# First layer's gate and up projections by seven quarter products, and the modulation as sets of four float32 products on TensorE

## Chip, cores and metric

The kernel runs on one core of a Trainium2 chip. The metric is device time in microseconds (us), the median of three runs; less is better.

## What is computed

One denoising step of a two-layer trunk on 512 latent and 128 context tokens (640 in all), width 1024, float32. Each layer first maps a conditioning vector to six modulation vectors of 1024 values, once for the latent tokens and once for the context tokens:

```python
sh1, sc1, g1, sh2, sc2, g2 = jnp.split(mod, N_MOD, axis=-1)
h = rmsnorm(x, prm['norm1_g'][l]) * (1 + sc1) + sh1
cols = jnp.einsum('bnd,de->bne', h, prm['w_in'][l])
...
mix = jnp.einsum('bne,ed->bnd', jnp.concatenate([ya, yb, yc], axis=-1), prm['w_out'][l])
x = x + g1 * mix
h = rmsnorm(x, prm['norm2_g'][l]) * (1 + sc2) + sh2
gate, up = jnp.split(jnp.einsum('bnd,df->bnf', h, prm['w_gu'][l]), 2, axis=-1)
x = x + g2 * jnp.einsum('bnf,fd->bnd', jax.nn.silu(gate) * up, prm['w_down'][l])
```

Here `mod` is SiLU(conditioning) times `w_mod` (1024 x 6144 in each layer) plus a bias. Between `cols` and `mix` lie the mixers: a chunked gated delta rule with a short convolution, a spatial-gating branch and a pooling branch. The FFN's hidden width is 2816, which is 22 blocks of 128.

## The kernel before

Activations are kept transposed: 128 channels on the partitions, the 640 tokens along the free axis, worked on in halves of 320. A float32 weight block is split into a rounded part (`wh`) and a rest (`wl`), and so is an activation (`xhi`, `xlo`); a product is three fp32r passes (`mm3`, line 338). Each pass of a block of 128 x 128 weights over one half is one instruction on TensorE. Where the text says a plain pass, it means that.

The stages follow one another: prologue (load, transpose, first two sixths of the modulation), mixer of layer 0, output projection of layer 0 (line 1303), FFN of layer 0 (from line 1314), then the same three for layer 1 and a final norm. Instructions are placed on the engines' queues before the run by a scheduler that goes by priorities (`PRI`, program order) and its own picture of time; at run time each engine takes its queue in order. TensorE's chains of projections are kept in order among themselves by `behind` (line 169), and everything else is put between them.

**The FFN.** In layer 0 all 22 blocks are done one by one: gate (8 weight blocks x 3 passes x 2 halves) and up (the same), 96 passes a block, then `w_down` in pieces of 8, 8 and 6 blocks. In layer 1 two blocks are done in this way (`unit_old`, line 1416), two on normalised rows (`unit_plain`, line 1442), and the other 18 by `Unit` (line 1465), which forms gate and up of a block from seven quarter products P1 to P7 of 12 passes each, on sums of rows (`t_sums`) and sums of weight blocks (`prep`): 84 passes. There the down projection goes in pieces of 4, 4, 4, 5 and 5 blocks (`PIECES`).

**The modulation.** The prologue computes the first two sixths of layer 0 by `first_mod_` (line 502): 8 float32 products [128 x 32] x [128 x 512] in four column groups of the array, then four transposes and a sum over the groups on VectorE. The other ten sixths are 20 groups of 512 columns, each in 8 steps (`pump`, line 256): a tile `wm` of `w_mod` (256 KB) is loaded by SyncE's queue, VectorE multiplies and adds it into `ma` for the latent tokens, ScalarE multiplies it for the context tokens and GpSimd adds that. After 8 steps `mod_sums` reduces `ma`: by 8 transposes on TensorE outside the FFN, by VectorE transposes and 4 small products in it. `PUMPS` and `POUT` say behind which projections a step goes. `pump_to` completes what a stage needs. The last group is finished about half way through the FFN of layer 0.

Of the kernel before, what the change touches and what calls it, by code (L numbers as in the profile page):

```python
# [9 lines left out]
F32 = mybir.dt.float32  # L10
# [29 lines left out]
W32, WM, WHL = 2, 3, 2  # L40
# [55 lines left out]
def tile_hybrid_step(ctx: ExitStack, tc: tile.TileContext,  # L96
# [115 lines left out]
    quarters = const.tile([P, 32], F32, name="quarters")  # L212
# [11 lines left out]
    steps = [(l, w * D + c0, k) for l, w in SIXTHS for c0 in (0, 512) for k in range(KT)]  # L224
    ps_ = {"i": 0, "j": 0, "ma": None, "wm": {}, "due": None, "at": "mix0"}

    def mod_sums(l, c0, ma):
        t0 = c0 // P
        if ps_["at"] != "ffn0":
            for s in range(2):  # L230
                pt = md()
                for cb in range(4):
                    nc.tensor.transpose(pt[:, cb * P:(cb + 1) * P], ma[:, s, cb * P:(cb + 1) * P], ident)
                m = mod[:, l, s, t0:t0 + 4]
                nc.vector.tensor_reduce(m, pt.rearrange("p (c n) -> p c n", c=4), op=ADD, axis=AX.X)
                tt(m, m, bmod[:, l, t0:t0 + 4], ADD)
            mod_scales(l, c0)
            return

        ms = sm.tile([P, 2, 16], F32, tag="ms", name="ms", bufs=1)  # L240
        for s in range(2):
            pt = md()
            nc.vector.transpose(pt, ma[:, s])
            nc.vector.tensor_reduce(ms[:, s], pt.rearrange("p (c n) -> p c n", n=32), op=ADD, axis=AX.X)
# [3 lines left out]
        tt(mod[:, l, :, t0:t0 + 4], pt[:, 0:8].rearrange("p (s t) -> p s t", s=2),  # L248
           bmod[:, l, t0:t0 + 4].unsqueeze(1).to_broadcast([P, 2, 4]), ADD)
        mod_scales(l, c0)  # L250
# [5 lines left out]
    def pump(n=1):  # L256
        with at("pump"):
            pump_(n)

    def pump_(n):  # L260
        for _ in range(n):
            if ps_["due"] is not None:
                mod_sums(*ps_["due"])
                ps_["due"] = None
            i = ps_["i"]
            if i >= len(steps):
                return
            while ps_["j"] < min(len(steps), i + WM):
                l, c0, k = steps[ps_["j"]]
                wm = wp.tile([P, 512], F32, tag="wm", name="wm", bufs=WM)  # L270
                nc.sync.dma_start(wm, w_mod[l, k * P:(k + 1) * P, c0:c0 + 512])
                ps_["wm"][ps_["j"]] = wm
                ps_["j"] += 1
            l, c0, k = steps[i]
            wm = ps_["wm"].pop(i)
            if k == 0:
                ps_["ma"] = sm.tile([P, 2, 512], F32, tag="ma", name="ma", bufs=1)
            ma = ps_["ma"]
            if k == 0:
# [6 lines left out]
            if k == KT - 1:  # L286
                ps_["due"] = (l, c0, ma)
            ps_["i"] += 1

    def pump_to(l, w):  # L290

        n = 2 * KT * (SIXTHS.index((l, w)) + 1)
        while ps_["i"] < n:
            pump()
        if ps_["i"] == n and ps_["due"] is not None:
            mod_sums(*ps_["due"])
            ps_["due"] = None
# [53 lines left out]
    def gemm_xs(wb, xs, evac, pumps=(1, 1), done=None):  # L351


        for half in range(2):
# [14 lines left out]
            pump(pumps[half])  # L369

    def gemm_act(wb, ks, xs, evac, n=1):
        wh, wl = wb
        for half in range(2):
            sl = slice(half * HALF, half * HALF + HALF)
            o = acc()[:, 0:HALF]
            for i, k in enumerate(ks):
                hi, lo = xs[i]
                mm3(o, wh[k], wl[k], hi[:, sl], lo[:, sl], i == 0, i == len(ks) - 1)
            evac(o, half)
            pump(n)  # L380
# [77 lines left out]

    wsp = tc.alloc_tile_pool(name="wsh", bufs=1, side="right")
    with tc.tile_pool(name="xin", bufs=1) as xp:  # L460
# [24 lines left out]
        def wm_tile():  # L485
            return wp.tile([P, 512], F32, tag="wm", name="wm", bufs=WM)

# [14 lines left out]
        def first_mod_(ws, c0, pool):  # L502
            pm = md()
            for k in range(KT):
                g = 32 * (k % 4)
                mm(pm[g:g + 32, :], sc[:, k, :], ws[k], k < 4, k >= KT - 4, tile_position=(0, g))
            msb = pool.tile([P, 512], F32, tag="msb", name="msb", bufs=1) if pool else wm_tile()
            copy("msb", msb, pm, "v")
            pt = md()
            for cb in range(4):  # L510
                nc.tensor.transpose(pt[:, cb * P:(cb + 1) * P], msb[:, cb * P:(cb + 1) * P], ident)
            m = mod[:, 0, :, c0 // P:c0 // P + 4]
            nc.vector.tensor_reduce(m, pt.rearrange("p (cb g m) -> p m cb g", cb=4, g=4)[:, 0:2], op=ADD, axis=AX.X)
            tt(m, m, bmod[:, 0, c0 // P:c0 // P + 4].unsqueeze(1).to_broadcast([P, 2, 4]), ADD)
# [43 lines left out]
        nc.vector.tensor_reduce(quarters, ident.rearrange("p (g m) -> p m g", g=4), op=ADD, axis=AX.X)  # L558
# [13 lines left out]
        for k in range(KT):  # L572
            xk = xks[k]
            if k % 2:
                sq = xp.tile([P, NT], F32, tag="sq", name="sq", bufs=1)
            else:
                sq = sm.tile([P, 2, 512], F32, tag="ma", name="sq", bufs=1).rearrange("p s n -> p (s n)")[:, 0:NT]
# [20 lines left out]
    for l in range(DEPTH):  # L598
        xs = nrm.xs
        with ExitStack() as es:  # L600
# [50 lines left out]
            def gemm_in(c0, n, evac, key):  # L651
                wb, done = early.pop(c0, None) or (wcol(c0, n), None)
                gemm_xs(wb, xs, evac, PUMPS.get(f"{key}{l}", (0, 1)), done)

# [484 lines left out]
            def pool():  # L1139
                mark(f"pool{l}")  # L1140
                pT = on[2:4]
                for i in range(2):
                    gemm_xs(wcol(C_PP + i * P, P), xs, ev_act(pT[i], AF.Identity), PUMPS.get(f"pool{l}", (0, 1)))
# [28 lines left out]
            def branches():  # L1172
# [3 lines left out]
                for i in range(2):  # L1176
                    gemm_xs(wcol(C_VB + i * P, P), xs, ev_act(vT[i], AF.Gelu_apprx_tanh), PUMPS.get(f"sgu{l}", (0, 1)))
# [23 lines left out]
                for i in range(2):  # L1201
                    gemm_xs(wcol(C_U + i * P, P), xs, ev_act(uT[i], AF.Gelu_apprx_tanh), PUMPS.get(f"sgu{l}", (0, 1)))
# [17 lines left out]
                for h in range(NH):  # L1220
                    gemm_xs(wcol(C_Z + h * P, P), xs, ev_act(zs[h], AF.Silu), PUMPS.get(f"z{l}", (0, 1)))
# [65 lines left out]
        if l + 1 < DEPTH:  # L1287
            with tc.tile_pool(name=f"fx{l}", bufs=1, reuse_waits="tile") as xpool, tc.tile_pool(name=f"ft{l}", bufs=1, reuse_waits="tile") as ftp, tc.tile_pool(name=f"ff{l}", bufs=1, reuse_waits="tile") as fp:
                x = [xpool.tile([P, NT], F32, name=f"x{k}") for k in range(KT)]
                for n in range(KT):  # L1290
                    nc.scalar.dma_start(x[n], xd[n])

                def ft(name):
                    return ftp.tile([P, NT], F32, tag="ft", name=name, bufs=4)

                ps_["at"] = f"out{l}"
                pump_to(l, 2)
                pump_to(l, 4)
                nrm = Norm(l, 1)
                for n in range(KT):  # L1300
                    cs = slice(n * P, (n + 1) * P)
                    wb = wblock([(w_out[l, 4 * P:8 * P, cs], 0, 4), (w_out[l, 0:4 * P, cs], 4, 4)], 8, P)
                    gemm_act(wb, range(8), yb + ya, resid(l, 16, n, x[n]), POUT)
                    nrm.add(n, x[n], ft("sq"), shift=False)
                pump_to(l, 3)
                for n in range(KT):
                    nrm.shift(n)
                rst = nrm.finish()
                xs2 = nrm.xs
                mark(f"ffn{l}")  # L1310
                ps_["at"] = f"ffn{l}"
                pieces = (8, 8, 6)
# [429 lines left out]
```

## Time and profile before

| | before |
|---|---|
| median of 3 runs | 1706.49 us (1705.74 to 1706.92) |
| profiled execution, its own time | 1703.07 us |
| span of its instructions | 1701.3 us |
| TensorE busy | 1633.1 us, 96% |
| VectorE busy | 1263.5 us, 74% |
| ScalarE busy | 827.8 us, 49% |
| GpSimd busy | 505.3 us, 30% |

The profiled execution lies 3.4 us under the median. PE is TensorE, DVE VectorE, ACT ScalarE, POOL GpSimd, SP SyncE (which only issues DMAs). A pass is shown with a duration of about 310 ns, but one starts every 147 ns: passes are pipelined, so costs on PE are read from start to start.

### The profile page before, as it was taken

How to read it: one execution, taken by the hardware profiler on the slowest of the kernel's cores; microseconds unless marked ns; L12 is line 12 of the kernel's file. 1: busy time of each engine (PE TensorE's matmuls, PEld its weight loads, DVE VectorE, ACT ScalarE, POOL GpSimd, SP SyncE). 2: the span in 40 equal slices, each digit the busy share in tenths (PEclk: the TensorE clock that was granted, in tenths of full speed). 3: DMA queues.
4: the chain of work that ended last, by engine and by line, in shares of the span. 5: the costliest groups of instructions: out<-in, count | busy, mean ns of one | idle time of the engine just before them, and what ended most of it. 6: DMA issues, size and time to landing. Idle time of an engine off the chain costs nothing.

```text
span 1701.3 us, 33005 instructions
## 1 busy us (share of the span) xinstructions
PE 1633.1 (96%) x12736; PEld 1567.5 (92%) x12736; DVE 1263.5 (74%) x2618; ACT 827.8 (49%) x1712; POOL 505.3 (30%) x533
## 2 busy tenths in 40 slices
PE   6999999998999999999999999999999999999997
PEld 4788989888899999999998989899999999999997
DVE  6688687789988778887556876776586768585774
ACT  4467765544444344434335756734363435353453
POOL 4342330356654645555146212111410000000000
PEclk8999999999999999999999999999999999999999
DMA  9431221444544544444234111113321323322331
GB/s 319 151 99 46 82 82 39 118 155 124 155 143 136 158 135 142 143 149 130 72 106 115 45 39 51 43 39 89 107 75 53 102 63 106 87 75 62 100 100 62
DMA packets 243636, 174.34 MB, mean 102 GB/s; under 512 B 10262, under 2 KB 212632, under 8 KB 243480
## 3 DMA queue, kind: packets, MB, share of 16 engines
q1 hardware_dynamic: 232144, 157.45, 30.7%
q10 hardware_dynamic: 10184, 12.29, 2.2%
q0 software_dynamic: 1152, 2.51, 0.5%
q8 instruction: 100, 1.64, 0.4%
q14 instruction: 56, 0.46, 0.1%
HBM read 163.29 MB, written 8.91 MB: 101 GB/s over the span
## 4 chain that ended last, share of the span: by engine, by line
PE 51%; DVE 3%; ACT 1%; issue 1%; DMA 1%; POOL 0%; DVEq 0%; ACTq 0%; POOLq 0%
PE acc L121 39%; PE dl L121 11%; PE md L121 0%; DMA w<-in_w_down_dram 0%; DVE wl L126 0%; DVE cv L129 0%; PE dl L1694 0%; DMA w<-in_w_gu_dram 0%; POOL guh L835 0%; PE md L765 0%; DVE yt L129 0%; DVE Z L126 0%; DVE st L129 0%; DVE dl L126 0%; ACT MT L950 0%
## 5 line engine op out<-in xcount | busy, mean ns | idle before, releaser
L121 PE MATMUL acc<-xhi,wh 128*128 128x322 f32 (+2 forms) x1472 | 468.5, 319 | 5.4 <-DVE ga L126 4.5
L121 PE MATMUL acc<-xlo,wh 128*128 128x322 f32 (+2 forms) x1472 | 466.6, 317 | 1.3 <-DVE xlo L129 1.2
L121 PE MATMUL acc<-xhi,wl 128*128 128x320 f32 (+1 forms) x1440 | 456.7, 317 | 4.9 <-DVE wl L126 4.9
L329 POOL TENSOR_TENSOR wl<-w,wh 128x384 fp32r<-128x384 f32 x128 | 172.3, 1346 | 832.1 <-ACT wh L325 429.7
L325 ACT CAST wh<-w 128x1024 fp32r<-128x1024 f32 (+3 forms) x186 | 179.4, 964 | 258.9 <-PE acc L121 184.3
L121 PEld LDWEIGHTS acc<-xhi,wh 128*128 128x128 f32 (+1 forms) x1472 | 278.6, 189 | 10.7 <-PE acc L121 7.2
L121 PEld LDWEIGHTS acc<-xlo,wh 128*128 128x128 f32 (+1 forms) x1472 | 278.7, 189 | 3.8 <-POOL wl L329 1.5
L121 PEld LDWEIGHTS acc<-xhi,wl 128*128 128x128 f32 x1440 | 275.1, 191 | 6.5 <-DVE wl L126 5.9
L285 POOL TENSOR_TENSOR ma<-ma,wm 128x512 f32<-128x512 f32 x140 | 206.6, 1476 | 134.3 <-ACT wm L154 115.0
L126 DVE TENSOR_TENSOR wl<-w,wh 128x640 fp32r<-128x640 f32 (+3 forms) x186 | 201.3, 1082 | 46.0 <-issue 19.8
L121 PE MATMUL acc<-ah,wh 128*128 128x320 f32 (+2 forms) x644 | 198.9, 310 | 0.5
L121 PE MATMUL acc<-al,wh 128*128 128x320 f32 (+2 forms) x644 | 198.4, 308 | 0.0
L121 PE MATMUL acc<-ah,wl 128*128 128x320 f32 (+2 forms) x644 | 198.3, 308 | 0.0
L154 ACT ACTIVATE wm<-wm,sc 128x512 f32<-128x512 f32 x140 | 101.0, 722 | 136.0 <-DVE ma L129 113.8
L129 DVE SCALAR_TENSOR_TENSOR x<-acc,mod,x 128x128 f32<-128x128 f32 (+3 forms) x240 | 97.3, 434 | 85.0 <-PE acc L121 84.7
L129 DVE SCALAR_TENSOR_TENSOR ma<-wm,sc,ma 128x512 f32<-128x512 f32 x140 | 138.4, 988 | 23.9 <-DMA wm<-in_w_mod_dram 23.1
L121 PEld LDWEIGHTS acc<-ah,wh 128*128 128x128 f32 x644 | 120.7, 188 | 1.7 <-DVE ga L126 1.2
L121 PEld LDWEIGHTS acc<-al,wh 128*128 128x128 f32 x644 | 120.8, 188 | 0.1
L121 PEld LDWEIGHTS acc<-ah,wl 128*128 128x128 f32 x644 | 120.8, 188 | 0.0
L1482 ACT CAST sh<-sv 128x512 fp32r<-128x512 f32 x72 | 44.5, 620 | 36.1 <-PE dl L121 15.4
L1328 ACT CAST ah<-ga 128x320 fp32r<-128x320 f32 x44 | 20.2, 460 | 82.3 <-DVE ga L129 82.3
L129 DVE SCALAR_TENSOR_TENSOR ga<-up,bt,ga 128x320 f32<-128x320 f32 (+2 forms) x66 | 59.3, 924 | 1.3
(432 smaller groups left out, 3537.6 us busy)
## 6 DMA issues: line engine op xcount, KB each, us to landing
wm<-in_w_mod_dram SPq DMA_DIRECT2D x162, 256.0 KB, 2.9
w<-in_w_gu_dram SPq DMA_DIRECT2D x70, 512.0 KB, 3.8
w<-in_w_in_dram SPq DMA_DIRECT2D x44, 512.0 KB, 3.6
wu<-in_w_gu_dram SPq DMA_DIRECT2D x18, 512.0 KB, 3.8
w<-in_w_out_dram SPq DMA_DIRECT2D x32, 256.0 KB, 3.0
w<-in_w_down_dram SPq DMA_DIRECT2D x16, 512.0 KB, 4.3
wf<-in_w_mod_dram SPq DMA_DIRECT2D x30, 256.0 KB, 5.7
w<-in_w_down_dram SPq DMA_DIRECT2D x24, 256.0 KB, 2.6
```

Source lines behind the costliest of these rows:

```text
L121: return nc.tensor.matmul(o, lhsT=l, rhs=r, start=st, stop=sp, **kw).ins
L126: recent["v"] = nc.vector.tensor_tensor(o, a, b, op=op).ins
L129: recent["v"] = nc.vector.scalar_tensor_tensor(o, a, s, b, op0=op0, op1=op1).ins
L154: recent["a"] = nc.scalar.activation(o, i, f, **kw).ins
L285: nc.gpsimd.tensor_tensor(ma[:, 1], ma[:, 1], wm, op=ADD)
L325: nc.scalar.copy(wh, v)
L329: nc.gpsimd.tensor_tensor(wl[:, c:], v[:, c:], wh[:, c:], op=SUB)
L1328: nc.scalar.copy(hi[:, sl], ga[:, sl])
L1482: nc.scalar.copy(hi, w)
```

## The change

Layer 0's FFN is now done by the code of layer 1: two blocks by `unit_old`, two by `unit_plain`, 18 by `Unit`, with the same pieces. The last piece of layer 0 ends in a down projection that also feeds the next norm, as before.

The 20 modulation groups are no longer multiplied on VectorE, ScalarE and GpSimd. A group is 8 float32 products on TensorE in two sets of four, one product in each of four column groups of 32 (the form of `first_mod_`). The copy of the result to SBUF (`msb`, VectorE) is followed by four small products with a 0/1 matrix of 2 columns, which add the four column groups and transpose in one, and one addition on VectorE. The prologue uses the same tail. There are four `wm` buffers now, so the second set of a group can be loaded only when the first set has read its tiles. Within a set the tile that was loaded last is taken first. Groups go behind the mixers' projections (0.18 of a group behind each half: 8 groups in the mixer of layer 0, 7 in that of layer 1) and behind P6 of every fourth block in layer 0's FFN (5 groups).

```diff
-POUT = 1
-
-PUMPS = {'log0': (0, 0), 'k00': (0, 0), 'q00': (1, 2), 'sgu0': (1, 1), 'z0': (0, 1), 'v10': (1, 1), 'q10': (0, 0), 'v00': (1, 0), 'k10': (0, 1), 'pool0': (1, 0)}
+
+SHARE = (0.18, 0.18)
...
-W32, WM, WHL = 2, 3, 2
+W32, WM, WHL = 2, 4, 2
...
+    def mod_columns(ws, l, c0, msb):
+
+        pm = md()
+        prev = None
+        for i in range(KT):
+            k, g = i, 32 * (i % 4)
+            if ws is None:
+                if i % 4 == 0:
+                    mod_loads(4)
+                    four = [ps_["wm"].pop(0) for _ in range(4)]
+                k = i + 3 - 2 * (i % 4)
+                w = four[k % 4]
+            else:
+                w = ws[k]
+            m = mm(pm[g:g + 32, :], sc[:, k, :], w, i < 4, i >= 4, tile_position=(0, g))
+            if ws is None and i % 4:
+                behind(m, prev)
+            prev = m
+        copy("msb", msb, pm, "v")
+
         pt = md()
-        for a in range(4):
-            mm(pt[32 * a:32 * a + 32, 0:8], quarters, ms.rearrange("p s (t a) -> p a s t", a=4)[:, a], True, True, tile_position=(0, 32 * a))
...
+        for cb in range(4):
+            mm(pt[:, 2 * cb:2 * cb + 2], msb[:, cb * P:(cb + 1) * P], C("I16")[:, 0:2], True, True)
+        tt(mod[:, l, :, c0 // P:c0 // P + 4], pt[:, 0:8].rearrange("p (t s) -> p s t", s=2),
+           bmod[:, l, c0 // P:c0 // P + 4].unsqueeze(1).to_broadcast([P, 2, 4]), ADD)
...
+    def mod_loads(n):
+
+        while len(ps_["wm"]) < n and ps_["j"] < KT * len(groups):
+            l, c0 = groups[ps_["j"] // KT]
+            k = ps_["j"] % KT
+            wm = wm_tile()
+            nc.sync.dma_start(wm, w_mod[l, k * P:(k + 1) * P, c0:c0 + 512])
+            ps_["wm"].append(wm)
+            ps_["j"] += 1
...
-            if k == 0:
-                behind_recent("v", ts, ma[:, 0], wm, sc[:, k, 0:1], None, MUL)
-                behind_recent("a", times, f"pump{ps_['at']}", ma[:, 1], wm, sc[:, k, 1:2], "a")
-            else:
-                behind_recent("v", stt, ma[:, 0], wm, sc[:, k, 0:1], ma[:, 0], MUL, ADD)
-                behind_recent("a", times, f"pump{ps_['at']}", wm, wm, sc[:, k, 1:2], "a")
-                nc.gpsimd.tensor_tensor(ma[:, 1], ma[:, 1], wm, op=ADD)
...
+    def pump(share):
+
+        ps_["sum"] += share
+        while ps_["sum"] >= 1.0 - 1e-6:
+            ps_["sum"] -= 1.0
+            if ps_["i"] < len(groups):
+                pump_group()
...
-        if l + 1 < DEPTH:
...
-                pieces = (8, 8, 6)
...
+                    if l + 1 < DEPTH and j % 4 == 0:
+                        pump_group()
...
+                if final:
+                    pump_to(l + 1, 1)
+                    pump_to(l + 1, 0)
+                    nrm = Norm(l + 1, 0)
...
+                    if final:
+                        nrm.add(n, x[n], xpool.tile([P, NT], F32, tag="sqn", name="sqn", bufs=2))
+                        nc.scalar.dma_start(xd[n], x[n])
```

In the rows of the queues below, `acc`, `dl` and `md` are PSUM tiles; `xhi`, `xlo`, `rh`, `rl`, `tah`, `tal` activations or row sums; `wh`, `wl`, `sh` weights or weight sums.

TensorE's queue in the FFN of layer 0, before: projections, and the small products at the end of a modulation group.

```order
L121 MATMUL acc<-xlo,wh 128x322
L121 MATMUL acc<-xhi,wl 128x322
L121 MATMUL md<-ms,quarters 32x8 x4
L121 MATMUL acc<-xhi,wh 128x320
L121 MATMUL acc<-xlo,wh 128x320
```

The same stage now, at the second set of a group of `wm`. Its first set of four stands 35 rows above it, behind a P6, with 34 passes between.

```order
L120 MATMUL acc<-tah,sl 128x320
L120 MATMUL acc<-tah,sh 128x320
L120 MATMUL md<-wm,sc 32x512 x4
L120 MATMUL acc<-tal,sh 128x320
L120 MATMUL acc<-tah,sl 128x320
L120 MATMUL dl<-rh_5063,sh 128x320
L120 MATMUL dl<-rl_5064,sh 128x320
L120 MATMUL dl<-rh_5063,sl 128x320
L120 MATMUL dl<-rh_5065,sh 128x320
L120 MATMUL md<-cst,msb 128x2 x4
```

The small products have made way for the float32 sets and for four products of 2 columns. A set does not always stay together. TensorE's queue in the mixer of layer 0, now, inside the delta rule's chain (`R`, `QK`):

```order
L120 MATMUL acc<-xhi,wl 128x320
L120 MATMUL md<-wm,sc 32x512
L120 MATMUL dl<-R,QK 128x128
L120 MATMUL md<-wm,sc 32x512
L120 MATMUL dl<-R,QK 128x128
L120 MATMUL md<-wm,sc 32x512
L120 MATMUL dl<-R,QK 128x128
L120 MATMUL md<-wm,sc 32x512
L120 MATMUL dl<-R,QK 128x128
```

Here the four products of a set stand singly, each with a full-width product behind it. Of the 40 sets, 26 stand whole, 13 as one product and three, and this one as four single ones: 56 stretches in all.

SyncE's queue in the FFN of layer 0, now:

```order
L1386 DMA wu<-in_w_gu_dram 128x8x128
L296 DMA w_6218<-in_w_gu_dram 128x8x128
L261 DMA wm<-in_w_mod_dram 128x512 x8
L1386 DMA wu<-in_w_gu_dram 128x8x128
L296 DMA w_6359<-in_w_gu_dram 128x8x128
```

The first four of the eight loads wait for the first set on TensorE, the next four for the second set; the weight loads of the next blocks are queued behind them. Before, three or four such loads stood between two weight loads, each waiting for GpSimd.

## Rows read from the trace of the kernel before

**Rows 1.** Busy time by stage: us, PE, PEld, DVE, ACT, POOL, clock, DMA
```profile
50.00:333.00 283.00, 270.14 (x2696) 254.29 (x2697) 226.28 (x598) 181.01 (x443) 90.77 (x116) 0.98 0.26 78
333.00:411.00 78.00, 69.61 (x431) 66.09 (x430) 67.01 (x91) 36.05 (x57) 46.87 (x37) 0.93 0.49 151
411.00:904.60 493.60, 481.12 (x3295) 473.61 (x3294) 384.17 (x604) 203.13 (x316) 253.32 (x196) 1.00 0.43 133
904.60:1183.50 278.90, 272.34 (x2732) 255.84 (x2730) 198.58 (x589) 163.06 (x404) 62.46 (x107) 1.00 0.19 53
1183.50:1246.00 62.50, 61.56 (x412) 59.54 (x411) 37.61 (x60) 23.98 (x40) 26.50 (x28) 1.00 0.36 110
1246.00:1646.20 400.20, 399.27 (x2710) 396.91 (x2710) 289.85 (x529) 181.03 (x330) 3.14 (x3) 1.00 0.29 82
```

**Rows 2.** TensorE's waits in layer 0's FFN: who for whom, us, times, longest
```profile
PE acc L121 <- DVE wl L126: 4.9, 3, 3.3
PE acc L121 <- DVE ga L126: 4.5, 7, 0.7
```

**Rows 3.** The same in layer 0's output projection, 333 to 411 us
```profile
PE md L233 <- POOL ma L285: 1.6, 1, 1.6
```

**Rows 4.** The same in layer 0's mixer, 50 to 333 us
```profile
PE dl L121 <- DVE Z L126: 3.3, 3, 2.6
PE dl L121 <- DVE W L129: 2.3, 1, 2.3
```

**Rows 5.** Costliest groups, page: busy, mean ns, idle before and releaser
```profile
L285 POOL TENSOR_TENSOR ma<-ma,wm 128x512 f32<-128x512 f32 x140 | 206.6, 1476 | 134.3 <-ACT wm L154 115.0
L129 DVE SCALAR_TENSOR_TENSOR ma<-wm,sc,ma 128x512 f32<-128x512 f32 x140 | 138.4, 988 | 23.9 <-DMA wm<-in_w_mod_dram 23.1
```

**Rows 6.** Chain that ended last, layer 1's FFN: start, us, what
```profile
1280.24 3.52 PE dl L121 x24
...
1385.41 25.34 PE acc L121 x171
```

**Rows 7.** TensorE's timeline in the prologue: start, us, line, tiles, shape, count
```profile
43.72 0.31 PE L121 MATMUL acc<-xhi,edT 128*128 128x320 f32 x1
43.97 1.92 PE L121 MATMUL md<-wf,sc 128*32 128x512 f32 x16
45.82 0.41 PE L121 MATMUL dl<-xhi,eon 128*128 128x320 f32 x1
46.07 0.31 PE L121 MATMUL dl<-xlo,eon 128*128 128x320 f32 x1
46.22 0.31 PE L121 MATMUL dl<-xhi,eon 128*128 128x320 f32 x1
...
46.66 1.02 PE L121 MATMUL dl<-ss,cst 128*128 128x512 f32 x2
47.52 0.60 PE L511 MATMUL md<-r_ident,wm 128*128 128x128 f32 x4
```

**Rows 8.** TensorE's timeline, small products in layer 0's mixer, first and last
```profile
69.43 0.31 PE L121 MATMUL dl<-g,cst 128*128 128x20 f32 x2
...
70.70 0.40 PE L121 MATMUL acc<-xhi,eon 128*128 128x322 f32 x1
```

**Rows 9.** TensorE's timeline, transposes of a modulation group in layer 0's mixer
```profile
309.83 1.04 PE L233 MATMUL md<-r_ident,ma 128*128 128x128 f32 x8
310.62 0.40 PE L121 MATMUL acc<-xhi,wh 128*128 128x322 f32 x1
```

**Rows 10.** The loads of wm: issue ns least/median/most, and us to landing
```profile
L271 SPq DMA_DIRECT2D wm<-in_w_mod_dram x160: 327/328/842, 50.1 to 794.6; - x160
...
DMA to landing us min/median/max: 2.7/2.9/7.3
```

**Rows 11.** The loads of wf in the prologue, many in flight: us to landing
```profile
DMA to landing us min/median/max: 4.2/5.7/7.2
```

**Rows 12.** TensorE's timeline in the prologue, 8 products that await their loads
```profile
22.82 5.23 PE L121 MATMUL md<-wf,sc 128*32 128x512 f32 x16
```

More of the change, by code (lines that the diff above doesn't have):

```diff
@@ L211, in tile_hybrid_step @@
     ident = rr["ident"].bitcast(F32)
-    quarters = const.tile([P, 32], F32, name="quarters")
     xd = [dram.tile([P, NT], F32, name=f"xd{k}") for k in range(KT)]
@@ new lines, in tile_hybrid_step @@
+    groups = [(l, w * D + c0) for l, w in SIXTHS for c0 in (0, 512)]
+    ps_ = {"i": 0, "j": 0, "wm": [], "sum": 0.0}
+    def mod_columns(ws, l, c0, msb):
[16 more added lines that the diff above has]
+        copy("msb", msb, pm, "v")
+        pt = md()
+        for cb in range(4):
+            mm(pt[:, 2 * cb:2 * cb + 2], msb[:, cb * P:(cb + 1) * P], C("I16")[:, 0:2], True, True)
+        tt(mod[:, l, :, c0 // P:c0 // P + 4], pt[:, 0:8].rearrange("p (t s) -> p s t", s=2),
+           bmod[:, l, c0 // P:c0 // P + 4].unsqueeze(1).to_broadcast([P, 2, 4]), ADD)
@@ L290, in pump_to @@
-    def pump_to(l, w):
[L292 to L297, printed above, removed]
+    def mod_loads(n):
[6 more added lines that the diff above has]
+            ps_["j"] += 1
@@ new lines, in wm_tile, with pump_group @@
+    def wm_tile():
+        return wmp.tile([P, 512], F32, tag="wm", name="wm", bufs=WM)
+    def pump_group():
+        with at("pump"):
+            l, c0 = groups[ps_["i"]]
+            mod_columns(None, l, c0, sm.tile([P, 512], F32, tag="msb", name="msb", bufs=1))
+            mod_scales(l, c0)
+            ps_["i"] += 1
+            mod_loads(4)
+    def pump(share):
[4 more added lines that the diff above has]
+                pump_group()
@@ L300, in wload @@
+    def pump_to(l, w):
+        while ps_["i"] < 2 * (SIXTHS.index((l, w)) + 1):
+            pump_group()
     def wload(parts, kn, n):
@@ L349, in mmk, with gemm_xs @@
         return mm3(o, wb[0][k], wb[1][k], hi[:, sl], lo[:, sl], k == 0, k == KT - 1)
-    def gemm_xs(wb, xs, evac, pumps=(1, 1), done=None):
+    def gemm_xs(wb, xs, evac, share=0.0, done=None):
         for half in range(2):
@@ L368, in gemm_xs, with gemm_act @@
                 evac(o, half, bt)
-            pump(pumps[half])
-    def gemm_act(wb, ks, xs, evac, n=1):
+            pump(share)
+    def gemm_act(wb, ks, xs, evac):
         wh, wl = wb
@@ L379, in gemm_act @@
             evac(o, half)
-            pump(n)
     def rsqrt(y, a, t):
@@ L456, in resid @@
         return f
+    wmp = tc.alloc_tile_pool(name="wmp", bufs=1, side="right")
     wsp = tc.alloc_tile_pool(name="wsh", bufs=1, side="right")
@@ L502, in first_mod_ @@
         def first_mod_(ws, c0, pool):
[L503 to L514, printed above, removed]
+            mod_columns(ws, 0, c0, sm.tile([P, 512], F32, tag="msb", name="msb", bufs=1))
         mark("mod00")
@@ L573, in tile_hybrid_step @@
             xk = xks[k]
[L574 to L577, printed above, removed]
+            sq = xp.tile([P, NT], F32, tag="sq", name="sq", bufs=2)
             if k < 2:
@@ L652, in gemm_in @@
                 wb, done = early.pop(c0, None) or (wcol(c0, n), None)
-                gemm_xs(wb, xs, evac, PUMPS.get(f"{key}{l}", (0, 1)), done)
+                gemm_xs(wb, xs, evac, SHARE[l], done)
             def cwt(name, tag):
@@ L1356, in ft @@
                 return ftp.tile([P, HALF], F32, tag="ft", name=name, bufs=NFT)
-            ps_["at"] = f"out{l}"
             pump_to(l, 2)
@@ L1372, in tile_hybrid_step @@
             mark(f"ffn{l}")
-            ps_["at"] = f"ffn{l}"
+            if l + 1 == DEPTH:
+                wmp.release()
             scoped.close()
@@ L1625, in tile_hybrid_step @@
                     unit_go(j, "P6")
+                    if l + 1 < DEPTH and j % 4 == 0:
+                        pump_group()
                     if nx:
@@ L1634, in tile_hybrid_step @@
                         unit_go(j, "P7")
-                        if not final:
+                        if not (final and l + 1 == DEPTH):
                             acts[j] = units[j].acts
@@ L1641, in tile_hybrid_step @@
                     acts[j] = units.pop(j).acts
-                if final:
+                if final and l + 1 == DEPTH:
                     break
@@ L1651, in tile_hybrid_step @@
                         Down(fn, [acts[j] for j in js], n, wdown(f0, fn, n)).go([(q, i) for q in range(2) for i in range(fn)])
+                    if final:
+                        nrm.add(n, x[n], xpool.tile([P, NT], F32, tag="sqn", name="sqn", bufs=2))
+                        nc.scalar.dma_start(xd[n], x[n])
                 f0 += fn
+            if l + 1 < DEPTH:
+                rst = nrm.finish()
+                scoped.close()
+                continue
             mark("final")
```

113 lines of the change are left out of this document (5 added, 108 removed).

## The prediction, made before the result was known

> **What bounds the kernel now.** I read the table of busy time by stage first [rows 1]. TensorE is busy for all but a few per cent in every stage, so a stage gets shorter only by work taken from TensorE or by waits of TensorE that go. The two layers compute the same thing, and the modulation is over before layer 1 begins: layer 1's stages are layer 0's without it. The output projection takes 78.0 us in layer 0 and 62.5 us in layer 1. The mixers take 283.0 and 278.9 us, with TensorE idle for 12.9 and 6.6 us and a clock of 0.98 and 1.00. The two FFNs, 493.6 us and 400.2 us plus a last piece, differ in their code too. The list of TensorE's waits then says who is late in layer 0: DVE's `wl` and `ga` in the FFN [rows 2], the pump's own GpSimd addition in the projection [rows 3], DVE in the inverse of the mixer [rows 4]. These are the engines that carry the pump: 206.6 us on GpSimd and 138.4 us on DVE [rows 5].
>
> Durations below are from start to start, since passes overlap. All is summed against the profiled execution: span 1701.3 us, its own time 1703.07 us, which is 3.4 us under the median of 1706.49. I add the difference to the median.
>
> **FFN of layer 0: minus 57.8 us, without its modulation groups.** It will be layer 1's code. Layer 1 needs 400.2 us up to the end of its last quarter products [rows 1]. There the down projection of the last piece is missing (layer 1 ends otherwise): 8 columns x 2 halves x 5 blocks x 3 = 240 passes at 25.34 / 171 = 0.148 us [rows 6], 35.6 us. Together 435.8 against 493.6. Counted in passes, 18 blocks lose 12 each: 216 at 0.147 (3.52 / 24) [rows 6] are 31.8 us. The other 26 us are what TensorE now loses to late splits and evacuations: 12.5 us idle alone, against 0.9 in layer 1 [rows 1, 2]. The cover for the added splits and sums of weights is DVE, 289.9 of 400.2 us busy in layer 1 [rows 1]. If DVE were late as often as now, the 26 us would be lost again; but the multiply-adds of the pump leave it, so I take all of it.
>
> **Output projection of layer 0: minus 15.5 us.** 78.0 to 62.5 [rows 1]. All groups that it needs are done in the mixer before it, and no step runs in it any more.
>
> **The sets on TensorE: plus 67 us.** The prologue shows eight such products [rows 7]. From the pass at 43.72 to the one at 46.22 it takes 2.50 us; three plain passes are 0.44 of it, which leaves 2.06 for 8 products. A full-width float32 stream of 512 columns takes (47.52 - 46.66) / 2 = 0.43 us, and a product needs two, so eight one behind the other would be 6.9: the four column groups do run side by side, 0.86 us a set, plus 0.34 us for getting in and out of the stretch. A whole set standing alone is then 1.20 us. The queue has 56 stretches. A single product still streams its 0.86 us, and a full-width product behind it has to wait for it. So 56 x 1.20 = 67.2 us. No row shows a set broken up. Below, the 16 extra stretches cost nothing, if they stand where TensorE waits anyhow (minus 19); above, each costs the full 1.20. I take 1.20, because the row between passes is the nearest.
>
> The price of 0.34 us is a row. The Trainium skill, "TensorEngine Tiling (Array Packing)", Key Properties, has the rule for it: changing the tiling mode drains TensorE. The trace agrees with those 0.34 us. Another rule speaks against the change: "TensorE: Matmul & The Clock Gate", the table under "Why this matters for your kernels", gives 2.38 times for three products of 32 columns side by side, not three. By that share a set would stream about 1.08 us, an estimate, and the sum below would come out 12 us higher. The trace disagrees: four take exactly the time of one.
>
> **The small products: plus 17 us.** Twelve instructions of 128 x 20 float32 take 70.70 - 69.43 = 1.27 us from first to last [rows 8], two to a product. A group has four products, eight instructions, 0.85 us; 20 groups, 17.0 us. The prologue has the same tail in place of four transposes of 0.11 us [rows 7]: plus 1 us with the DVE sum that goes.
>
> **What else goes.** Three of the six groups done before the FFN were reduced in layer 0's mixer, by 8 transposes each, (310.62 - 309.83) = 0.79 us [rows 9]: minus 2.4. The other three are in the projection's difference, the rest in the FFN's.
>
> **Waits in the mixer of layer 0: minus 12 us.** If it waits as layer 1's does, idle falls by 12.9 - 6.6 = 6.3, and the clock from 0.98 to 1.00 gives back 2% of 283, 5.7 us [rows 1]. The clock's low level of 1.2 GHz came behind such waits of over 2 us [rows 4]. Bounds: nothing, or all 12.9 + 5.7 = 18.6.
>
> **The new wait: loads of the second set, plus 3 us.** With four buffers, the loads of a second set are issued when the first has been read. Each issue takes 0.33 us and a lone load lands 2.9 us after it [rows 10]. Eight products that awaited their loads took 5.23 us [rows 12], so tiles arrive some 0.65 us apart. From the start of the first set: about 1.0 until the tiles are read, 2.9 to the first landing, 3 x 0.65 for the others: 5.9 us. The set itself takes 0.9 and the 34 passes behind it 34 x 0.147 = 5.0. In front of the second set TensorE thus waits about 0.1 us, with 4 fewer passes 0.6. I take 0.15 x 20. Below, nothing. Above, tiles land as in the prologue with many loads in flight, 5.7 us [rows 11]; the last is then 1.8 us late each time, 36 us. Who waits for TensorE then: evacuations and splits of the next block, hardly late in layer 1. Queued behind these loads on SP are weights of the next blocks, held for up to 6 us; a block lasts 84 x 0.147 = 12.3 us and its weights are loaded a block ahead, so I cost this at nothing. First sets are loaded one group ahead.
>
> **Sum.** -57.8 - 15.5 + 67.2 + 17.0 + 1 - 2.4 - 12 + 3 = +0.5 us. The work taken from three engines with time to spare is put on the one that has none, and it costs about what the quarter products bring. Median: 1706.49 + 0.5 = **1707.0 us**. By stage: FFN 0 454 us with its five groups (12 stretches), output projection 62.5, mixer 1 about 308 (7 groups, 20 stretches), mixer 0 about 303.
>
> **Rivals.**
>
> 1. **The sets fill TensorE's waits; faster.** 44 of the 56 stretches lie in the mixers, where the two had 19.5 us of idle in all, and the broken sets stand in chains of the delta rule, where a product waits for DVE. If the 16 extra stretches cost nothing there (19.2) or the left idle of 6.6 us a mixer is used, 10 to 22 us come off: about 1691. For it: a product put where TensorE would stand is free. Against it: most idle is in few long waits, and the queue's order is fixed before the run.
> 2. **Second sets wait for their loads, or the longer queue delays the chains; slower.** One mechanism: TensorE stands at the second set in 20 places, all later passes behind it. It decides once the last of four tiles lands over 3.9 us after its issue; at 0.9 us each it is 18 us, about 1722, more if the clock falls behind the waits. For it: 5.7 us to landing in the prologue, and weight loads between the four on SP in the mixers. Against it: 2.9 us at the median while the queue was as full.
> 3. **The products don't run side by side.** If each starts when its own tile lands, eight take 5.23 instead of 1.92 us [rows 7, 12]: 20 x 3.3 = 66, 1773 us. Against it: the tile loaded last is awaited first.
>
> **How the numbers follow.** A measurement of this kernel can tell about 0.2%, 3.4 us, from no change. The sum as worked out: 44%, spread over 1698 to 1715, of which 24 parts are within 0.2%, 10 faster, 10 slower. Rival 1: 29%. Rival 2: 25%. Rival 3: 2%. Faster 0.39, same 0.24, slower 0.37. The unknown costs' bounds together reach from 1707 - 19 - 6.6 - 3 = 1678 to 1707 + 12 + 33 = 1752, but not at once on one side; 1687 to 1723 holds the sum's spread and most of rivals 1 and 2, and leaves out about 2 in 10.
>
> **What would show it.** FFN of layer 0: 18 blocks at 12.3 us and no wait on `wl`; between 449 and 459 us in all. Sets: four starts within 0.03 us, two levels 0.43 apart, 1.2 us from pass to pass. Mixer 1 longer by 25 to 32 us, else rival 1. In TensorE's list of waits, DMA `wm` under 5 us in all, else rival 2. The prediction is wrong if layer 0's FFN keeps its waits, if single products don't hold up the passes behind them, or if the mixers' chains lose more than they are given.

## The result, and the profile after

The changed kernel takes 1732.01 us (median of 4 runs, 1729.16 to 1732.99) against 1706.38 us: a ratio of 1.0142, with an interval of 1.0125 to 1.0159. I had forecast 1707, and a range up to 1723. The profiled execution has a span of 1730.5 us, 29.2 more than before, where my sum was plus 0.5.

By stage, in the form of [rows 1] (us, then busy time and instructions of PE, PEld, DVE, ACT and POOL, granted clock, DMA share, GB/s): mixer, output projection and FFN of layer 0, then the mixer and output projection of layer 1.

```profile
50.00:372.09 322.09, 308.21 (x2875) 266.34 (x2874) 197.29 (x572) 158.41 (x410) 56.34 (x97) 0.96 0.31 93
372.09:442.40 70.31, 66.77 (x430) 62.46 (x429) 39.06 (x63) 24.88 (x39) 26.26 (x28) 0.98 0.38 118
442.40:900.03 457.63, 454.73 (x3084) 440.19 (x3082) 315.94 (x588) 197.37 (x358) 12.15 (x23) 1.00 0.35 103
900.03:1213.48 313.45, 302.44 (x2901) 265.11 (x2898) 208.82 (x605) 160.35 (x402) 62.64 (x107) 1.00 0.31 91
1213.48:1275.83 62.35, 61.41 (x411) 59.38 (x410) 37.51 (x60) 23.90 (x39) 26.40 (x28) 1.00 0.36 111
```

Against [rows 1] the FFN of layer 0 has lost 36 us and its output projection 8. The two mixers have grown by 39 and 34.5. My stage forecasts were 454 for the FFN, 62.5 for the projection, 303 and 308 for the mixers. Against them the mixer of layer 0 is 19 us long, the projection behind it 8, the mixer of layer 1 5 and the FFN 4. That is more than the 28.7 us by which the sum was missed, since the stage figures were rounded down and hold neither the 3 us of loads nor the 1 us of the prologue. In the mixer of layer 0 TensorE is idle for 322.1 - 308.2 = 13.9 us, not less than the 12.9 of before, and its clock has fallen from 0.98 to 0.96.

The sets cost what [rows 7] had promised. The first piece is TensorE's timeline in the mixer of layer 0 at a whole set of four (two instructions to a product, eight in a row of the view), the second a set that is broken into single products, with one product of the delta rule behind each (start, us, line, tiles, shape, count).

```profile
341.64 0.31 PE L120 MATMUL acc<-xhi,wl 128*128 128x322 f32 x1
341.88 1.06 PE L120 MATMUL md<-wm,sc 128*32 128x512 f32 x8
342.88 0.41 PE L120 MATMUL acc<-xhi,wh 128*128 128x320 f32 x1
...
303.33 1.04 PE L120 MATMUL md<-wm,sc 128*32 128x512 f32 x2
304.30 0.49 PE L120 MATMUL dl<-R,QK 128*128 128x128 f32 x2
304.72 1.04 PE L120 MATMUL md<-wm,sc 128*32 128x512 f32 x2
305.70 0.49 PE L120 MATMUL dl<-R,QK 128*128 128x128 f32 x2
```

From the set's start to the next instruction it is 1.00 us for four products and 0.97 us for a single one. So a single product does hold up the queue as long as a whole set. Between passes a whole set takes 342.88 - 341.64 = 1.24 us, 0.147 of which is the pass itself, so 1.09 us are added (I had 1.20).

TensorE's waits for the loads of `wm` (who for whom, us, times, longest):

```profile
PE md L120 <- DMA wm<-in_w_mod_dram: 7.0, 12, 1.4
```

And their landing, in the form of [rows 10]:

```profile
DMA to landing us min/median/max: 2.7/3.5/8.1
```

I had set 3 us for them; in my text, over 5 us would speak for rival 2.

### The profile page after: what moved, and what is told of

Read it like the earlier page. It is cut to its first block, busy times and chain, and to the rows that moved or that the text cites. A ratio compares the mean times of both kernels' runs of the same rounds, so it can differ in the third digit from the quotient of the medians.

```text
span 1730.5 us, 32562 instructions
## 1 busy us (share of the span) xinstructions
PE 1669.8 (96%) x12856; PEld 1552.5 (90%) x12856; DVE 1147.4 (66%) x2561; ACT 785.1 (45%) x1702; POOL 207.8 (12%) x325
## 4 chain that ended last, share of the span: by engine, by line
PE 85%; DVE 6%; DMA 4%; ACT 2%; issue 1%; POOL 1%; SPq 1%; ACTq 0%; DVEq 0%
PE acc L120 56%; PE dl L120 21%; PE md L120 6%; DMA wm<-in_w_mod_dram 3%; SPq L261 1%; PE md L737 1%; DVE wl L125 1%; POOL guh L807 0%; ACT wh L315 0%; DVE yt L128 0%; DMA w<-in_w_down_dram 0%; PE md L1094 0%; DVE cv L128 0%; PE dl L1619 0%; DVE st L128 0%
## 5 line engine op out<-in xcount | busy, mean ns | idle before, releaser
L315 ACT CAST wh<-w 128x1024 fp32r<-128x1024 f32 (+2 forms) x184 | 164.1, 892 | 359.2 <-PE acc L120 231.4
L120 PE MATMUL acc<-xhi,wh 128*128 128x320 f32 (+3 forms) x832 | 268.3, 323 | 2.2 <-DVE wh L125 0.8
L120 PE MATMUL acc<-xlo,wh 128*128 128x320 f32 (+3 forms) x832 | 268.9, 324 | 1.2 <-DVE xlo L128 1.2
L120 PE MATMUL acc<-xhi,wl 128*128 128x320 f32 (+1 forms) x800 | 257.4, 322 | 0.2 <-DVE wl L125 0.2
L120 PEld LDWEIGHTS acc<-xhi,wh 128*128 128x128 f32 (+1 forms) x832 | 157.8, 190 | 14.3 <-issue 7.7
L120 PEld LDWEIGHTS acc<-xlo,wh 128*128 128x128 f32 (+1 forms) x832 | 157.8, 190 | 10.6 <-issue 7.4
L120 PEld LDWEIGHTS acc<-xhi,wl 128*128 128x128 f32 x800 | 154.1, 193 | 3.8 <-issue 3.0
L125 DVE TENSOR_TENSOR sl<-sv,sh 128x512 fp32r<-128x512 f32 x144 | 99.2, 692 | 8.8 <-ACT sh L1394 5.8
L120 PE MATMUL acc<-tbh,sh 128*128 128x320 f32 x288 | 89.2, 310 | 0.0
L120 PE MATMUL acc<-tbl,sh 128*128 128x320 f32 x288 | 89.0, 309 | 0.0
```

What stands on the lines that cost most here:

```text
L120: return nc.tensor.matmul(o, lhsT=l, rhs=r, start=st, stop=sp, **kw).ins
L125: recent["v"] = nc.vector.tensor_tensor(o, a, b, op=op).ins
L315: nc.scalar.copy(wh, v)
```

## The experiments

**1. No groups at all.** The kernel leaves out the loads, products and sums of all 20 groups; the vectors that they would give are zero. It gives the bare stages.

```diff
     def pump_group():
-        with at("pump"):
-            l, c0 = groups[ps_["i"]]
-            mod_columns(None, l, c0, sm.tile([P, 512], F32, tag="msb", name="msb", bufs=1))
-            mod_scales(l, c0)
-            ps_["i"] += 1
-            mod_loads(4)
+        ps_["i"] += 1
```

> The changed kernel without its 20 modulation groups: neither their loads nor their products nor their sums; the vectors they would give are zero (the two sixths of the prologue are computed). It gives the bare time of each stage. Theory A: the waits and the low clock in the mixer of layer 0 belong to that stage itself, so the 12 us of my sum were never there to be had: without groups it still takes 280 to 290 us from 50 us to the first pass of the output projection, idle 9 us or more, clock 0.98 or less; about 1643 us in all. Theory B: the float32 sets and the small products of two columns, put into the chains of the delta rule, bring waits and low clock of their own in place of the pump's: without them the stage takes 270 to 277 us with a clock of 1.00 and about 6.6 us of idle, as layer 1's does; about 1631 us in all. Either way the FFN of layer 0 should take about 436 us (my term), the output projection 62.5 and the mixer of layer 1 279.

It took 1622.45 us (one run, span 1620.4). The stages, layer 0's three and layer 1's mixer:

```profile
50.00:321.27 271.27, 264.87 (x2705) 250.33 (x2705) 186.41 (x558) 155.99 (x409) 54.82 (x97) 1.00 0.18 50
321.27:385.56 64.29, 62.53 (x410) 60.76 (x409) 37.57 (x60) 23.94 (x39) 26.32 (x28) 0.97 0.35 107
385.56:822.17 436.61, 435.83 (x2963) 433.79 (x2962) 311.69 (x576) 197.39 (x358) 12.20 (x23) 1.00 0.29 84
822.17:1102.32 280.15, 272.23 (x2732) 255.54 (x2730) 199.73 (x589) 163.16 (x404) 64.57 (x107) 1.00 0.19 53
```

Theory B holds: without groups the mixer of layer 0 takes 271.3 us, idle for 6.4, at a clock of 1.00 (in all it takes 9 us less than the theory had). So the gain that I had counted on exists, and the groups take it back. All 20 together cost 1730.5 - 1620.4 = 110.1 us, 5.5 each; my terms for them came to 87. Stage by stage they cost 50.8 us in the mixer of layer 0, 6.0 in its projection, 21.0 in the FFN (5 groups) and 33.3 in the mixer of layer 1 (7 groups).

**2 and 3. Each part alone.** Quarter products with the old pump (the calls of the new FFN code, shortened):

```diff
                     unit_go(j, "P6")
+                    if l + 1 < DEPTH:
+                        pump(UP[0])
                     if nx:
                         unit_go(nx, "P2")
+                        if l + 1 < DEPTH:
+                            pump(UP[1])
...
                     unit_go(j, "P4")
+                    if l + 1 < DEPTH:
+                        pump(UP[2])
```

> One part alone: layer 0's FFN by quarter products, but the modulation by the old steps on VectorE, ScalarE and GpSimd, three steps to a block of Unit and one behind each down projection of a column. My sum: minus 57.8 us in the FFN if VectorE keeps up, so about 1650 us. Rival: VectorE (290 us busy in layer 1's FFN, plus about 110 us of multiply-adds here) is late with sums and splits as in the kernel before, the 26 us of waits stay, and only the passes are saved: 1675 us. The mixer and output projection of layer 0 stay at 283 and 78 us in both.

And the sets with the old FFN of layer 0, a group behind every fourth block:

```diff
                         gemm_xs(wblock([(w_gu[l, :, FF + j * P:FF + (j + 1) * P], 0, KT)], KT, P), xs2, evu)
+                        if j % 4 == 3:
+                            pump_group()
                         acts.append((hi, lo))
```

> The other part alone: the modulation as sets on TensorE, but layer 0's FFN by the old code with a group behind every fourth block. If the 26 us of waits in that FFN come from the pump's work on VectorE, the old FFN takes 468 us plus 18 us of groups and the kernel about 1760 us. If they come from the old code itself (two splits a block, pieces of 8), it takes 494 plus 18 and the kernel about 1785 us. Mixers as in the changed kernel in both (322 and 313 us).

Quarter products alone took 1721.21 us (ratio 1.0092, 1.0068 to 1.0115), sets alone 1765.64 us (1.036, 1.0339 to 1.0381). Each part alone makes the kernel slower, by 16 and 61 us, and both together by 26. The FFN of layer 0 with quarter products and the old pump:

```profile
410.79:918.36 507.57, 466.56 (x3069) 447.87 (x3067) 474.25 (x762) 267.30 (x470) 170.69 (x129) 0.97 0.44 130
```

And with the old code and the sets:

```profile
436.54:930.77 494.23, 487.86 (x3300) 475.55 (x3299) 213.00 (x426) 129.40 (x204) 111.50 (x90) 1.00 0.32 96
```

With the pump left on it, VectorE is busy for 474 of 507.6 us and TensorE idle for 41, at a clock of 0.97: the quarter products gain nothing, and the stage is even 14 us longer than before. VectorE's multiply-adds in that stage, in the form of [rows 5]:

```profile
L130 DVE SCALAR_TENSOR_TENSOR ma<-wm,sc,ma 128x512 f32<-128x512 f32 x98 | 103.9, 1061 | 8.1 <-DMA wm<-in_w_mod_dram 7.8
```

What TensorE waits for there:

```profile
PE acc L122 <- DVE ga L127: 6.0, 4, 2.2
PE acc L122 <- DVE sl L127: 6.0, 7, 1.9
PE acc L122 <- DVE x L130: 5.1, 5, 2.9
```

Sums of weights (`sl`), evacuations (`ga`) and residual additions (`x`) come late. So the rival of that run was right, and too small: 1721 where it had 1675. In the other kernel the old FFN takes 494 us with 5 groups; less the 21 us that 5 groups cost in the new code, that is 473 where I expected 468. If the groups cost as much in the old code, the 26 us of waits of the FFN before were the pump's, all but about 5.

**4. Sets kept whole.** The second to fourth product of a set get a priority that puts them right behind the first: 41 stretches instead of 57 (the prologue's one included).

```diff
+            if ws is None and i % 4:
+                tc.cur_priority -= 100000
             m = mm(pm[g:g + 32, :], sc[:, k, :], w, i < 4, i >= 4, tile_position=(0, g))
             if ws is None and i % 4:
+                tc.cur_priority += 100000
                 behind(m, prev)
```

> The changed kernel with the products of a set put on TensorE's queue one right behind the other: 41 stretches instead of 57. If a single product holds up the queue as long as a whole set (1.0 us from its start to the next start in the trace of the changed kernel), 16 stretches less are 16 to 18 us: about 1714 us. Rival: the broken sets stand where TensorE waits for the delta rule's chain anyhow: under 4 us, about 1729 us.

1704.56 us, ratio 0.9993 (0.9983 to 1.0002): 27 us better than the changed kernel (25 by the ratios, as the two were measured apart), where I expected 16 to 18, and no slower than before. The mixer and the projection of layer 0, then the FFN and the mixer of layer 1:

```profile
50.00:352.59 302.59, 289.10 (x2876) 257.70 (x2875) 195.35 (x572) 156.54 (x409) 56.08 (x97) 1.00 0.32 99
352.59:422.47 69.88, 66.71 (x430) 62.51 (x429) 39.12 (x63) 24.87 (x39) 26.32 (x28) 0.98 0.38 118
422.47:876.10 453.63, 452.24 (x3083) 439.92 (x3082) 315.76 (x588) 197.39 (x358) 12.15 (x23) 1.00 0.35 104
876.10:1189.10 313.00, 298.08 (x2901) 267.12 (x2898) 208.62 (x605) 160.24 (x402) 64.34 (x107) 0.99 0.31 91
```

Sixteen stretches at 1.0 to 1.09 us are 16 to 17 us, as expected. The rest is mostly clock in these two executions: layer 0's mixer has it at 1.00 here and had 0.96, which is about 12 us (summed over windows of 1 us), and 3.4 us are lost again in the mixer of layer 1. There what TensorE had less to do came back as waits: 14.9 us idle, 11.0 in the changed kernel. Over all executions the mean clock is 0.986 to 0.990 in the changed kernel and 0.987 to 0.993 here, so it is not shown that whole sets as such keep the clock.

**5 to 7. Sets spaced, spaced and whole, and the tail of the prologue before.** In the first the two sets of a group go behind different projections, and VectorE adds them; the second keeps each set whole as well; the third also reduces by four transposes.

```diff
-            mod_columns(None, l, c0, sm.tile([P, 512], F32, tag="msb", name="msb", bufs=1))
...
+            if h == 0:
+                ps_["msb"] = sm.tile([P, 512], F32, tag="msb", name="msb", bufs=1)
+                copy("msb", ps_["msb"], pm, "v")
+            else:
+                tt(ps_["msb"], pm, ps_["msb"], ADD)
+                mod_tail(l, c0, ps_["msb"])
```

> The changed kernel with the two sets of a group taken apart: each set goes behind a projection of its own (0.36 of a set behind each half, a set behind P6 of every second block), its sum over the two sets is done by VectorE, so that the four loads of a set have twice the time. Sets are still broken up (56 stretches). If TensorE's 12 waits for wm (7.0 us in the changed kernel's list of waits) come from the loads of the second set only, they go: about 1723 us. Rival: the loads are late for another reason (SyncE's queue order), the waits stay: about 1730 us.

> Both at once: sets whole and spaced. From the whole sets (1704.6 us) TensorE's 11 waits for wm, 9.7 us, go, and with them the low clock that followed the 2.1 us wait in the mixer of layer 1 (3.4 us of span): 1692 to 1695 us. If the waits go but as much is lost to the delta rule's chains, 1702 to 1705 us. If broken sets, and not the loads, are what lowers the clock in the mixer of layer 0, that stage keeps its clock of 1.00 here and has 0.98 or less in the run with spaced but broken sets.

> The run before with the tail undone: in place of the four float32 products of two columns, 0.85 us a group on TensorE, the four transposes of 0.11 us and the sum over the column groups on VectorE that the prologue had. My term for the small products (17.0 us) less 20 x 0.44 gives minus 8 us: about 1686 us. Rival: TensorE waits for VectorE's longer tail, or the transposes open a wait of their own: no gain, 1694 us.

They took 1723.56 us (1.010, 1.0085 to 1.0115), 1698.88 us (0.9956, 0.9940 to 0.9972) and 1697.07 us (0.9944, 0.9925 to 0.9963), all on one chip. The first met its expectation, the second lies between its own and the price of its rival. TensorE's waits for `wm` in the first:

```profile
PE md L120 <- DMA wm<-in_w_mod_dram: 1.2, 2, 0.6
```

In the second:

```profile
PE md L120 <- DMA wm<-in_w_mod_dram: 1.2, 2, 1.0
```

From 12 waits to 2: these waits were in the main those of second sets for their loads (in the changed kernel 10 of the 12, 6.2 of the 7.0 us, stand at second sets). Spacing brought 8 us with broken sets and 6 with whole ones; wholeness brought 25 us again. The tail brought 1.8 us where I expected 8, inside the uncertainty. In the profiled executions it brought about 8 us in the FFN of layer 0 and the mixer of layer 1 (450.3 to 448.6 and 311.0 to 304.5), and lost 4 in the mixer of layer 0 (304.7 to 308.7), whose idle time rose from 10.7 to 16.4 us. Most of that rise is one wait: the first set of the stage stands 4.0 us for its load, where it stood 1.0 us, and low clock around it costs 1.7 us more; why the load comes later is not shown. My third expectation of the second run fell: that mixer loses clock with whole sets too. The mixer of layer 0 with spaced sets:

```profile
50.00:364.54 314.54, 300.91 (x2898) 263.99 (x2898) 204.30 (x584) 161.86 (x413) 55.01 (x97) 0.98 0.33 100
```

With spaced whole sets:

```profile
50.00:354.73 304.73, 294.08 (x2895) 261.75 (x2894) 200.98 (x583) 157.27 (x410) 53.83 (x97) 0.99 0.34 102
```

With the transposes as well:

```profile
50.00:358.72 308.72, 292.35 (x2853) 257.99 (x2851) 200.00 (x593) 160.65 (x412) 54.30 (x97) 0.98 0.34 104
```

With groups in it the stage is idle for 10.7 to 16.9 us in all of these kernels (16.9 with the sets alone), against 6.4 without, whether sets are whole or not. Whole sets save their stretches; the waits come with the groups.

**8 and 9. The groups elsewhere.** The first of these moves 9 groups from the mixers into the FFN. The second takes the six groups left in the mixer of layer 0 away from the delta rule, behind the stage's last projections; in its trace eight of their 12 sets start after the delta rule's last product (281 us), four still stand among its steps.

```diff
-SHARE = (0.18, 0.18)
+SHARE = (0.135, 0.0)
...
                     gemm_xs(wblock([p_], KT, P, 0), xs2, ev)
+                    if l + 1 < DEPTH:
+                        pump_set()
...
-                    if l + 1 < DEPTH and j % 2 == 0:
+                    if l + 1 < DEPTH and ps_["i"] < len(groups):
                         pump_set()
```

> Sets whole and spaced with the tail of transposes, and 14 of the 20 groups in the FFN of layer 0 (a set behind every projection of the first four blocks, behind every P6 and behind four P5), 6 in the mixer of layer 0, none in the mixer of layer 1. By the stages of the spaced whole sets against the kernel without groups a group cost 2.7 us in the FFN (13.7 for 5) and 4.4 us in the mixers (66 for 15). If the price goes with the stage, 9 groups moved are minus 15 us: 1681 to 1684 us, the FFN of layer 0 at about 474 us, the mixer of layer 1 back at 280 us. Rival: with the loads of wm between all loads of weights on SyncE's queue, weights come late and the FFN pays 4.4 us a group too: about 1697 us.

```diff
-SHARE = (0.135, 0.0)
+SHARE = (0.31, 0.0)
...
-                gemm_xs(wb, xs, evac, SHARE[l], done)
+                gemm_xs(wb, xs, evac, 0.0, done)
```

> The run before with the 6 groups of layer 0's mixer moved within it: 0.31 of a group behind each half of the pooling, gating and z projections alone, none behind the q, k, v and log projections, so that its first 200 us hold no set and the last 50 us most of them. If the waits and the low clock that groups brought to this stage come from sets standing in front of the delta rule's chains, they go: the stage takes 271 (without groups) plus 6 x 2.7 to 3.2 (the price in the FFN), 288 to 291 us where it took 299.4, and the kernel about 1683 us. Rival: any schedule of this stage with groups in it waits 11 to 17 us and loses clock somewhere: the stage stays at 296 us or more, about 1691 us.

1692.68 us (0.9911, 0.9894 to 0.9927) and 1687.52 us (0.9877, 0.9858 to 0.9896), each against the kernel before on the same chip. The first lies between its expectation and its rival. The mixer and the FFN of layer 0 in the first:

```profile
50.00:349.43 299.43, 285.84 (x2798) 257.43 (x2794) 195.93 (x583) 156.54 (x409) 56.17 (x90) 0.97 0.30 91
...
414.08:894.90 480.82, 474.80 (x3244) 444.35 (x3242) 333.79 (x636) 198.66 (x358) 12.15 (x23) 1.00 0.44 136
```

The mixer of layer 0 in the second:

```profile
50.00:338.05 288.05, 278.28 (x2793) 253.60 (x2785) 193.18 (x580) 155.72 (x410) 54.50 (x92) 0.99 0.30 92
```

The price of a group goes with its place. In experiment 6, against the bare stages, eight whole spaced groups cost 33.5 us in the mixer of layer 0, 4.2 each, seven cost 30.8 in that of layer 1, 4.4 each, and five cost 13.7 in the FFN, 2.7 each, whose line there is:

```profile
420.98:871.32 450.34, 449.50 (x3067) 438.74 (x3066) 317.83 (x591) 197.70 (x358) 12.15 (x23) 1.00 0.34 103
```

In the first of these two kernels 14 groups in the FFN cost 480.8 - 436.6 = 44.2 us, 3.2 each, where I expected 2.7 (6 us are waits for `wm`; there is now a set to nearly every projection). Its six groups in the mixer of layer 0 cost 28.2 us, but 4.9 of these are one wait, that of the stage's first set for its load, and 3.4 more are half clock around it, from 58.5 to 65.3 us. Without both it is 3.3 us a group. The wait in TensorE's timeline:

```profile
59.59 1.94 PE L120 MATMUL md<-wm,sc 128*32 128x512 f32 x8 [4.88 <-DMA wm<-in_w_mod_dram]
```

The same six moved to the end of the stage cost 288.05 - 271.27 = 16.8 us, 2.8 each: idle time falls from 13.6 to 9.8 us, and the clock is back at 0.99. The theory had 288 to 291, its rival 296 or more. Two things weaken this. Eight of the 11 us between the two stages are that wait and its clock, not the delta rule's steps. And the stages are cut at 50 us, while the prologue's last products start at 54.8 us in the bare kernel and at 51.7 here; counted from there, the six cost 19.9 us, 3.3 each. The profiled execution of the first kernel lies 6 us above its median, and by the medians the last step is worth 5 us, not the 11 of the two stages. The last kernel is 1.2% faster than the kernel before.

## Why the prediction was wrong, step by step

The trace after and the kernel without groups split the sum in two.

- **FFN of layer 0, minus 57.8.** Bare it takes 436.6 us, minus 56.7. Right, and for the reason given: VectorE is at 312 of 437 us, and no wait on `wl` is left. That the pump must go for this is shown by experiment 2, where VectorE is busy for 474 of 507.6 us with it; which part of the pump matters was not tried.
- **Output projection, minus 15.5.** Bare 64.3, minus 13.9. With the groups it was minus 7.9: one set with its wait for a load and one tail run in it, where I had all of them done before it (some 2 us are left over). Both kernels have a low clock behind TensorE's wait of about 2 us for ScalarE's copy of `mixvn`, 1.7 us.
- **Sets, 67.2, and small products, 17.0.** 56 stretches at 1.09 us are 61 us, and eight small instructions take 0.81 to 0.94 us, 17 us for 20 groups. Right in size. A rule of the Trainium skill, "TensorEngine Tiling (Array Packing)", Key Properties, says that a change of the tiling mode drains TensorE; the trace agrees in that a stretch adds 1.09 us, more than the 0.86 us of its stream [rows 7].
- **Loads of the second set, 3.** 7.0 us, right in kind, too small by half. Tiles landed after 3.5 us at the median, where I had taken the 2.9 of the kernel before.
- **Waits in the mixer of layer 0, minus 12: the step that failed.** I took it that the stage would wait as layer 1's does once the pump was off VectorE, and that the groups would only add their own length. The first half holds: bare, idle time falls by 6.5 us and the 5.1 us of low clock go, 11.6 of the 12 that I counted. The second half does not. With groups in it, it is idle for 13.9 instead of 6.4 us and has a clock of 0.96 instead of 1.00: 7.5 and about 12 us, 20 us that no term of the sum held. Together with the 23 stretches and 7 tails of this stage (25 and 6 us) that accounts for its 50.8 us. The groups in the mixer of layer 1 brought 3 us of idle time.

These waits of TensorE in the mixer of layer 0 stand in the changed kernel and not in the kernel without groups:

```profile
PE md L120 <- DMA wm<-in_w_mod_dram: 1.7, 4, 0.7
PE md L737 <- ACT jk L153: 1.5, 3, 0.7
PE dl L120 <- DVE g L128: 1.2, 1, 1.2
PE md L120 <- DVE yy L128: 1.0, 1, 1.0
PE dl L120 <- DVE W L128: 0.8, 1, 0.8
PE md L120 <- DVE msb L150: 0.7, 1, 0.7
```

The first and the last, 2.4 us, are for the groups' own loads and copies. The other 4.5 us are for results of the mixer itself that come late from ScalarE and VectorE; what delays each of them was not traced.

So the sum of plus 0.5 missed by 6 us in the bare kernel, by 4 in the loads and by 20 in the mixer of layer 0 (1 or 2 of the loads' waits are among these), less 6 where sets were cheaper than I had them; some 5 us are spread over the rest.

**The rivals.** The first, sets that fill waits, is refuted by the two pieces of timeline and by experiment 4: each broken set cost its stretches in full, and waits grew. The second named the right place (the longer queue delays the chains), but I had priced it by the loads alone, at 18 us, and left the low clock as a remark; with the 12 us of clock it would have reached 1734. None of the three falls of the clock in that mixer (at 90, 141 and 261 us) stands behind a wait for a load. The third is refuted. I gave the second 25% and cut the range at 1723, just above it.

What stays open is which wait lets the clock fall. The kernel with the sets alone has TensorE's queue in the mixer of layer 0 in the same order as the changed kernel, and took 319.15 us there at a clock of 0.98, against 322.09 at 0.96. So the loss is not set by the order of the queue alone. That groups in this stage bring waits is shown. That it is their place among the delta rule's steps is less firmly shown: without the waits for `wm`, the stage is idle for 9.5 to 13.1 us in the kernels with seven or eight groups in it, 7.7 in experiment 8 with six, and 6.7 in experiment 9, where most of the six stand behind these steps; bare it is 6.4. How many of the 12 us of clock a given order loses is not shown: experiment 9 loses 3.4 us of it from 130 to 137 us, where no set stands.

## What to carry to other kernels

Work that moves to the engine with the least room should be priced twice: by its length, and by what it does to the chains it stands in front of; here the same group cost 2.7 to 3.3 us behind plain projections and 4.2 to 4.4 us in the mixers with their recurrence (experiment 6). A stretch of sets had one price, 0.97 us for a single product and 1.00 for four, so keep what belongs together in one piece of the queue. And a forecast for "this stage will be like its twin" should be split into the bare stage and what is newly put into it.

## What the runs showed of the hardware

The clock of TensorE fell behind shorter waits, and stayed low longer, than in [rows 4]. In the kernel before it stood at half for 3.4 us behind the wait of 2.6 us and for 6.8 us behind that of 2.3 us:

```profile
116.70:120.10 3.40, 3.40 (x15) 3.40 (x14) 3.40 (x11) 2.06 (x4) 1.35 (x4) 0.50 0.73 225
249.80:256.60 6.80, 6.80 (x176) 5.69 (x174) 6.73 (x12) 5.30 (x11) 5.03 (x4) 0.50 0.40 120
```

In the mixer of layer 0 of the changed kernel these are the two waits at a fall, which comes at 141.4 us, within the second of them (TensorE's timeline, in brackets the idle time and what ended it), and passes behind them that start 0.27 us apart instead of 0.147:

```profile
137.93 0.86 PE L120 MATMUL dl<-W,SI 32*32 32x16 f32 x80 [0.83 <-DVE W L128]
...
141.96 0.23 PE L120 MATMUL dl<-W 32*32 32x16 f32 x1 [1.47 <-issue]
...
142.56 0.47 PE L120 MATMUL acc<-xhi,wh 128*128 128x320 f32 x1
142.82 0.47 PE L120 MATMUL acc<-xlo,wh 128*128 128x320 f32 x1
```

The stretch by engines, in the form of [rows 1]: the clock is at 0.50, which is 1.2 GHz, for 10 us in which TensorE is busy for 9.54.

```profile
141.50:151.50 10.00, 9.54 (x168) 6.66 (x169) 5.04 (x11) 5.00 (x11) 1.64 (x1) 0.50 0.01 2
```

The other long fall of that stage has no wait of more than 0.7 us in the 5 us before it:

```profile
260.90:271.10 10.20, 10.02 (x232) 8.12 (x221) 3.78 (x11) 4.77 (x13) 0.63 (x1) 0.50 0.20 70
```

In the kernel without groups a wait as long as the 1.47 us above, in the same stage (TensorE's list of waits, the last number) brought no fall:

```profile
PE dl L120 <- issue: 1.8, 2, 1.5
```
